# Four more gate columns computed by seven-product jobs ahead of the attention, eight instead of twelve computed directly inside it

## The chip, the cores and the metric

The kernel runs on one core of a Trainium2 chip. A core has five engines that run their own instruction streams in order and wait for each other on semaphores: PE (matrix multiply, 128x128, into eight PSUM banks), DVE (vector), ACT (scalar functions, copies, casts), POOL (GpSimd) and SP, which here only issues DMAs. The metric is the device time of one execution in microseconds (us); lower is better.

## The reference, cut to what matters

One decoder block, sequence 1024, width 1024, all in float32. The parts that matter here:

```
proj = xn @ w_in                       # (1024, 5136): q, k, v of two branches, code, gate_sb, gate_gla
o_sb  = stick_breaking_attention(...)  # 8 heads x 64, causal, blocks of 128 rows
o_gla = gla_chunked(...)               # 4 heads, then a norm and a swish gate
y = sigmoid(gate_sb + b_gate[0]) * (o_sb @ w_branch_sb) \
  + sigmoid(gate_gla + b_gate[1]) * (o_gla @ w_branch_gla)
h = x + y @ w_out                      # then a gated convolutional FFN and a last norm
```

The two merge gates are 2048 columns of `w_in`: sixteen "gates" of 128 columns each, numbered 0 to 15 (0 to 7 belong to the attention branch, 8 to 15 to the GLA branch). Each is a product of a 1024x128 weight with the 1024x1024 input, a bias and a sigmoid. The gates are needed only when the branches are merged, so they can be computed at any time before that.

## The kernel before, in words

Every float32 operand is split into a high and a low part of a rounded type (`split`, L118: a cast on ACT, then a subtraction on DVE at L110), and each product is three matmuls of these parts (`mac`, L189 to L197; every matmul of it is L195). The input is held transposed in four quarters, "11", "12", "21", "22" (512 rows of time by 512 of width).

Two ways lead to a gate.

- A **seven-product job** (`fast`, L225 to L303) computes two weights of 128 columns at once. It replaces the eight products of 512x512 blocks by seven, at the price of sums and differences of the weights (`first_pieces`, `more_pieces`) and of the products (the `add`s, L116) on DVE. A job is 7 x 12 = 84 matmuls of 128x512. The pairs come from `project_pairs` (L439): two pairs of GLA queries and keys, four of attention queries and keys, two of the swish gate, and then the first `N_GATES` of the sixteen gates, two by two. This is the stage of the pairs. In it a job's gate leaves over the sigmoid of L516, both halves at once.
- A **direct gate** (`gates`, L524 to L555) computes one weight of 128 columns in the plain way: two halves of time, each 24 matmuls in four steps of 6, then a sigmoid (L552) and a store (L553). It is a generator; each `fill(gate_steps, 1)` issues one step. The weights of a gate are cast and split once, or twice for the first `N_HALVES` = 3, whose two halves are computed far apart.

```
446        for g in range(0, N_GATES, 2):
447            yield tuple((C_GATE + n * P, gate_d, n * P) for n in (g, g + 1))
531        gs = range(N_GATES, 2 * NK)
532        order = [(g, (0,)) for g in gs[:N_HALVES]]
533        order += [(g, (0, 1)) for g in gs[N_HALVES:]] + [(g, (1,)) for g in gs[:N_HALVES]]
739    for w in attend():
740        owed += w + EACH
741        while owed >= FILL:
742            owed -= FILL
743            fill(gate_steps, 1)
939    fill(gate_steps, BEFORE)
```

The attention (`attend`, L687) runs in four rounds of two heads. A round goes through four quarters `tp` = 0 to 3; a quarter handles 256 rows of time for both heads, so its work grows with `tp`: 2, 4, 6 and 8 blocks of 128 keys. For a chunk of up to four blocks, `weigh` makes the logits on PE (L654), a sigmoid on ACT (L656), a mask on POOL where the chunk holds the diagonal (L658), and a running product from the right on DVE (L661, a scan). `turn_weights` transposes the result on PE (L668) and splits it (L119 on ACT, L110 on DVE); `gather` multiplies it with the values on PE (L677), ends with a bias on ACT (L682) and an add on DVE (L116), and stores. Chunks are transposed up to six chunks or twelve blocks after they were weighed. The first round also loads and splits the values (`value_blocks`, with POOL's L643) and reloads the quarter "21" of the input (`whole21`, L590, casts at L598).

The order of the instructions is fixed when the program is built. The attention hands out one step of a direct gate for each `FILL` blocks weighed, and in the second to seventh chunk of the first round one more each (`MORE`, L724). The matmuls of a step have a lowered priority (`LATER`, L545), and the scheduler that lays out PE's stream puts them between those of the attention. What is left over is issued after the attention (L939, L949), ahead of and between the first matmuls of `branch`, which multiplies the attention's output by `w_branch_sb` (L870) and reads the gates back.

Of the kernel before, what the change touches and what calls it, by code (L numbers as in the profile page):

```python
# [34 lines left out]
C_GATE = 3088  # L35
T2 = 11
T4 = 14
FILL = 3.6
EACH = 0
LATER = 25  # L40
MORE = 1
# [11 lines left out]
GLA = 2, 3  # L53
PACES = 0, 0, 0, 1
EARLY = 6
N_GATES = 4
AT_END = 51
N_READY = 1
N_OPS = 11
# [6 lines left out]
def block_kernel(ctx: ExitStack, tc: tile.TileContext, x, norm_mix_g, w_in, b_gate, w_alpha_up, b_alpha,  # L66
# [97 lines left out]
    def fill(steps, n):  # L164
        for _ in range(n):
            next(steps, None)
# [272 lines left out]
    def project_pairs():  # L439
# [4 lines left out]
        for j in range(0, 4, 2):  # L444
            yield tuple((C_GR + n * P, gr_d, n * P) for n in (j, j + 1))
        for g in range(0, N_GATES, 2):
            yield tuple((C_GATE + n * P, gate_d, n * P) for n in (g, g + 1))
# [76 lines left out]
    def gates():  # L524
# [5 lines left out]

        gs = range(N_GATES, 2 * NK)
        order = [(g, (0,)) for g in gs[:N_HALVES]]
# [206 lines left out]
    for w in attend():  # L739
        owed += w + EACH  # L740
        while owed >= FILL:
            owed -= FILL
            fill(gate_steps, 1)
# [528 lines left out]
```

## Time and profile before

| | us |
|---|---|
| median of 3 runs (lowest, highest) | 1415.81 (1415.05, 1417.85) |
| the profiled execution | 1416.46 |
| its span in the trace | 1414.7 |
| PE busy in the span | 1383.0 (98%) |
| DVE busy | 1061.3 (75%) |
| ACT busy | 650.7 (46%) |
| POOL busy | 108.2 (8%) |

The stage of the pairs begins at 113 us of the span and ends at 311 us with the first matmuls of the attention; the attention's last gather ends at 550 us. A busy PE is not yet a full one: matmuls overlap in the array, so that a 128x512 matmul is on record with some 390 ns while a stream of them takes less than 230 ns each. How full PE is, is read from how many matmuls pass in a stretch.

### The profile page before, as it was taken

How to read it: one execution, taken by the hardware profiler on the slowest of the kernel's cores; microseconds unless marked ns; L12 is line 12 of the kernel's file. 1: busy time of each engine (PE TensorE's matmuls, PEld its weight loads, DVE VectorE, ACT ScalarE, POOL GpSimd, SP SyncE). 2: the span in 40 equal slices, each digit the busy share in tenths (PEclk: the TensorE clock that was granted, in tenths of full speed). 3: DMA queues.
4: the chain of work that ended last, by engine and by line, in shares of the span. 5: the costliest groups of instructions: out<-in, count | busy, mean ns of one | idle time of the engine just before them, and what ended most of it. 6: DMA issues, size and time to landing. Idle time of an engine off the chain costs nothing.

```text
span 1414.7 us, 18378 instructions
## 1 busy us (share of the span) xinstructions
PE 1383.0 (98%) x6577; PEld 1143.1 (81%) x6577; DVE 1061.3 (75%) x1642; ACT 650.7 (46%) x1246; POOL 108.2 (8%) x190
## 2 busy tenths in 40 slices
PE   7999999998899999999999999999999999999997
PEld 6788888886788888878888788888888888888886
DVE  6387776766888876647446997998888987896765
ACT  6234334645766665643234543343333333554654
POOL 0000000003311110300000000000000000000000
PEclk9999999999999999999999999999999999999999
DMA  6332234376624436565324344564554437953332
GB/s 249 129 109 77 79 113 136 126 198 205 169 86 124 119 122 203 201 214 174 103 105 138 100 120 149 179 208 149 179 177 150 149 106 267 321 176 102 98 103 101
DMA packets 158397, 212.67 MB, mean 150 GB/s; under 512 B 9771, under 2 KB 103021, under 8 KB 157793
## 3 DMA queue, kind: packets, MB, share of 16 engines
q1 hardware_dynamic: 139696, 155.46, 35.8%
q0 software_dynamic: 11312, 41.48, 7.7%
q10 hardware_dynamic: 7296, 14.55, 2.8%
q8 instruction: 52, 0.85, 0.2%
q14 instruction: 41, 0.33, 0.1%
HBM read 153.65 MB, written 57.80 MB: 149 GB/s over the span
## 4 chain that ended last, share of the span: by engine, by line
PE 70%; DVE 2%; ACT 1%; issue 0%; DVEq 0%; ACTq 0%
PE bank L195 42%; PE bank L1135 15%; PE bank L1002 5%; PE bank L677 2%; PE bank L654 2%; PE bank L668 2%; DVE t L110 1%; DVE t L116 1%; PE bank L808 1%; PE bank L771 0%; PE bank L843 0%; PE bank L795 0%; PE bank L820 0%; PE bank L319 0%; DVE t L311 0%
## 5 line engine op out<-in xcount | busy, mean ns | idle before, releaser
L195 PE MATMUL bank<-t,t 128*128 128x512 f32 x3648 | 867.2, 393 | 3.6 <-DVE t L110 1.5
L195 PEld LDWEIGHTS bank<-t,t 128*128 128x128 f32 x3648 | 681.1, 188 | 150.4 <-DVE t L110 2.7
L110 DVE TENSOR_TENSOR t<-t,t 128x512 fp32r<-128x512 f32 (+2 forms) x651 | 430.3, 694 | 83.3 <-ACT t L119 78.1
L119 ACT CAST t<-t 128x512 fp32r<-128x512 f32 x537 | 311.1, 620 | 308.7 <-DVE t L110 67.7
L116 DVE TENSOR_TENSOR t<-bank,t 128x512 f32<-128x512 f32 (+1 forms) x284 | 182.8, 653 | 124.0 <-PE bank L195 60.5
L1135 PE MATMUL bank<-t,t 128*128 128x512 f32 x924 | 209.6, 389 | 0.0
L1135 PEld LDWEIGHTS bank<-t,t 128*128 128x128 f32 x924 | 173.4, 188 | 36.0
L110 DVE TENSOR_TENSOR t<-t 128x512 f32<-128x512 f32 (+1 forms) x124 | 88.0, 718 | 5.3 <-DMA t<-in_w_ffn_in_dram 3.5
L366 PE MATMUL bank<-t,t 128*128 128x512 f32 x384 | 91.4, 396 | 0.0
L1002 PE MATMUL bank<-t,t 128*128 128x512 f32 x384 | 88.9, 391 | 0.0
L110 DVE TENSOR_TENSOR t<-bank,t 128x512 fp32r<-128x512 f32 (+4 forms) x128 | 72.1, 576 | 22.2 <-ACT t L119 21.8
L1033 ACT ACTIVATE t<-t,vcol 128x1024 f32<-128x1024 f32 x22 | 27.4, 1245 | 128.0 <-DVE t L116 128.0
L366 PEld LDWEIGHTS bank<-t,t 128*128 128x128 f32 x384 | 72.4, 191 | 15.5 <-DVE t L110 0.4
L1002 PEld LDWEIGHTS bank<-t,t 128*128 128x128 f32 x384 | 71.6, 188 | 14.7
L116 DVE TENSOR_TENSOR t<-t,t 128x512 f32<-128x512 f32 x107 | 69.9, 684 | 16.1 <-ACT t L471 15.4
L119 ACT CAST t<-bank 128x512 fp32r<-128x512 f32 (+3 forms) x124 | 61.6, 510 | 40.7 <-PE bank L319 19.4
L661 DVE TENSOR_TENSOR_SCAN t<-t,zero 128x128 f32<-128x128 f32 (+1 forms) x64 | 54.5, 861 | 23.4 <-POOL t L658 23.2
L1035 DVE SCALAR_TENSOR_TENSOR t<-t,vcol,t 128x1023 f32<-128x1023 f32 (+1 forms) x44 | 56.2, 1278 | 14.1 <-ACT t L1033 13.9
L654 PE MATMUL bank<-t,t 128*128 128x128 f32 (+3 forms) x192 | 55.7, 368 | 1.6 <-DVE t L110 1.6
L668 PE MATMUL bank<-ident,t 128*128 128x128 f32 x288 | 52.2, 275 | 3.1 <-DVE t L661 1.2
L658 POOL TENSOR_SCALAR_AFFINE_SELECT t<-t 128x128 f32<-128x128 f32 x64 | 34.2, 540 | 192.2 <-ACT t L656 184.0
L677 PE MATMUL bank<-t,t 128*128 128x256 f32 (+1 forms) x320 | 45.8, 277 | 2.7 <-ACT t L119 1.9
(126 smaller groups left out, 768.4 us busy)
## 6 DMA issues: line engine op xcount, KB each, us to landing
t<-in_w_ffn_in_dram SPq DMA_DIRECT2D x50, 512.0 KB, 4.1
t<-in_w_in_dram SPq DMA_DIRECT2D x43, 512.0 KB, 5.3
act_d<-t POOLq DMA_DIRECT2D x22, 512.0 KB, 5.7
t<-in_w_ffn_out_dram SPq DMA_DIRECT2D x22, 512.0 KB, 5.5
wsum_d<-t POOLq DMA_DIRECT2D x22, 512.0 KB, 4.4
t<-act_d SPq DMA_DIRECT2D x22, 512.0 KB, 5.7
t<-wsum_d SPq DMA_DIRECT2D x44, 256.0 KB, 3.3
t<-sqk_d SPq DMA_DIRECT2D x40, 256.0 KB, 4.2
```

The source lines that it names most:

```text
L110: nc.vector.tensor_tensor(out=o, in0=a, in1=b, op=ALU.subtract)
L116: nc.vector.tensor_tensor(out=o, in0=a, in1=b, op=ALU.add)
L119: nc.scalar.copy(h, src)
L195: nc.tensor.matmul(pt, a[:, kk], b[:, kk], start=start and kk == 0 and m == 0, stop=stop and kk == k - 1 and m == 2)
L366: nc.tensor.matmul(pt, a[:, k % 4, t], b, start=k == 0 and m == 0, stop=k == NK - 1 and m == 2)
L654: nc.tensor.matmul(z[:, 0:w], q[:, a, e, ts_], kk[:, e, b0 * P:b1 * P], start=a == 0, stop=a == 1)
L661: nc.vector.tensor_tensor_scan(out=kr, data0=kr, data1=zero.to_broadcast([P, w]), initial=1.0 if right is None else right[:, 0:1], op0=ALU ...
L668: nc.tensor.transpose(pt[:, b * P:(b + 1) * P], ke[:, b * P:(b + 1) * P], ident)
L677: nc.tensor.matmul(po[:, c0:2 * P], vt[b][:, head, :], a[b // 4][:, b % 4, c0:], start=(b == 0 and n == 0), stop=(b == nb - 1 and n == 1))
L1002: nc.tensor.matmul(pt, a[:, k % 4, t], b, start=(k == 0 and m == 0), stop=(k == NK - 1 and m == 2))
L1035: nc.vector.scalar_tensor_tensor(out=cv[:, i:], in0=av[:, :S - i], scalar=col(V_CW, (2 - i) * NF + f), in1=cv[:, i:], op0=ALU.mult, op1=AL ...
L1135: nc.tensor.matmul(pts[m][i], a[:, t], b, start=(k == 0 and x_ == 0), stop=(k == NH - 1 and x_ == 2))
```

## The change

`N_GATES` goes from 4 to 8: gates 4 to 7 join gates 0 to 3 as pairs, so the stage of the pairs has twelve jobs instead of ten, and eight direct gates are left instead of twelve. `FILL` goes from 3.6 to 5.6, so that the fewer steps are spread over the whole attention. A direct gate has 48 matmuls (two halves of 24), so four of them have 192; two jobs have 168.

```diff
-FILL = 3.6
+FILL = 5.6
...
-N_GATES = 4
+N_GATES = 8
```

In steps of six matmuls: before, 97 steps (the first of which only loads), of which the attention hands out 88 and 8 are left for behind it; in the changed kernel 65, with 58 and 6. On the other engines the program as a whole has 28 more additions and subtractions of 128x512 on DVE, and on ACT six more casts, two more copies, four more sigmoids of 128x1024 and eight fewer of 128x512. SP's DMAs are the same in number.

The first place to look at is PE between two rounds of the attention, from the last gather of the second round (L677) to the first gather of the third. L668 are transposes, L654 logits, L195 here steps of a direct gate. Before:

```order
L677 MATMUL bank_4081<-t_673_3771,t_516_2990 128x128
L195 MATMUL bank_4020<-t_474_2799,t_680_3815 128x512
L195 MATMUL bank_4020<-t_475_2800,t_680_3815 128x512
L195 MATMUL bank_4020<-t_474_2799,t_680_3815 128x512
L668 MATMUL bank_4103<-ident,t_708_3955 128x128
L195 MATMUL bank_4020<-t_474_2799,t_680_3815 128x512
L195 MATMUL bank_4020<-t_475_2800,t_680_3815 128x512
L195 MATMUL bank_4020<-t_474_2799,t_680_3815 128x512
L654 MATMUL bank_4107<-t_654_3671,t_679_3806 128x512 x2
L668 MATMUL bank_4126<-ident,t_710_3971 128x128 x2
```

In the changed kernel, at the same place:

```order
L677 MATMUL bank_4229<-t_708_3955,t_558_3238 128x128
L668 MATMUL bank_4251<-ident,t_739_4118 128x128
L654 MATMUL bank_4255<-t_688_3859,t_714_3990 128x512 x2
L668 MATMUL bank_4274<-ident,t_741_4128 128x128 x2
L677 MATMUL bank_4279<-t_724_4049,t_458_2825 128x256
```

The attention's own matmuls stand in the same order; the six matmuls of a direct gate between them are gone. Counted over the whole attention, from its first logits to its last gather, there are 524 matmuls of direct gates before and 355 in the changed kernel. By rounds that is 174, 120, 120, 110 before and 126, 78, 72, 79 in the changed kernel; by quarters, 73, 29, 43, 29 against 54, 24, 25, 23 in the first round, 19, 24, 48, 29 against 6, 23, 25, 24 in the second, 19, 28, 44, 29 against 6, 19, 29, 18 in the third and 19, 24, 48, 19 against 13, 17, 31, 18 in the fourth.

The second place is PE behind the attention, where the last direct steps meet the first matmul of `branch` (the L195 row with a new bank and new weights at the end of each piece). L771 belongs to the GLA's states. Before:

```order
L195 MATMUL bank_5423<-t_474_2799,t_983_5361 128x512
L771 MATMUL bank_5455<-t_975_5333,t_974_5331 128x256
L195 MATMUL bank_5423<-t_475_2800,t_983_5361 128x512
L195 MATMUL bank_5423<-t_474_2799,t_983_5361 128x512 x2
L195 MATMUL bank_5423<-t_475_2800,t_983_5361 128x512
L195 MATMUL bank_5423<-t_474_2799,t_983_5361 128x512 x2
L195 MATMUL bank_5423<-t_475_2800,t_983_5361 128x512
L195 MATMUL bank_5423<-t_474_2799,t_983_5361 128x512 x2
L195 MATMUL bank_5423<-t_475_2800,t_983_5361 128x512
L195 MATMUL bank_5423<-t_474_2799,t_983_5361 128x512
L195 MATMUL bank_5423<-t_55_320,t_984_5364 128x512
L195 MATMUL bank_5466<-t_986_5382,t_999_5420 128x512
```

In the changed kernel:

```order
L195 MATMUL bank_5402<-t_516_3057,t_985_5327 128x512 x2
L195 MATMUL bank_5402<-t_517_3058,t_985_5327 128x512
L195 MATMUL bank_5402<-t_516_3057,t_985_5327 128x512
L195 MATMUL bank_5402<-t_55_320,t_986_5330 128x512
L195 MATMUL bank_5402<-t_56_321,t_986_5330 128x512
L195 MATMUL bank_5402<-t_55_320,t_986_5330 128x512 x2
L195 MATMUL bank_5402<-t_56_321,t_986_5330 128x512
L195 MATMUL bank_5402<-t_55_320,t_986_5330 128x512 x2
L195 MATMUL bank_5486<-t_1003_5415,t_1016_5453 128x512
```

Between the last gather and that first matmul of `branch` stand 41 matmuls of direct gates before and 24 in the changed kernel; behind it, before the branch is alone with the GLA, 11 and 5 more.

## Rows read from the trace of the kernel before

**Rows 1.** The page: busy time and share of the span.

```profile
PE 1383.0 (98%) x6577; PEld 1143.1 (81%) x6577; DVE 1061.3 (75%) x1642; ACT 650.7 (46%) x1246; POOL 108.2 (8%) x190
```

**Rows 2.** The page: the chain that ended last, by engine.

```profile
PE 70%; DVE 2%; ACT 1%; issue 0%; DVEq 0%; ACTq 0%
```

**Rows 3.** Windows: pairs, four rounds, tail; start:end us, length, busy by engine, PEclk.

```profile
113.00:311.00 198.00, 198.00 (x869) 160.95 (x867) 139.63 (x227) 92.19 (x145) 10.82 (x20) 1.00 0.40 118
311.10:393.50 82.40, 72.28 (x403) 59.08 (x402) 63.00 (x89) 52.52 (x108) 27.24 (x32) 1.00 0.65 190
393.50:447.10 53.60, 53.60 (x321) 46.53 (x321) 44.20 (x65) 35.80 (x79) 7.96 (x16) 1.00 0.38 104
447.10:500.70 53.60, 53.60 (x323) 46.52 (x321) 44.33 (x66) 32.80 (x75) 8.81 (x16) 1.00 0.39 114
500.70:550.00 49.30, 49.26 (x295) 42.39 (x294) 34.68 (x53) 28.62 (x65) 3.75 (x9) 1.00 0.45 142
550.00:568.30 18.30, 18.30 (x82) 15.11 (x81) 9.49 (x18) 9.43 (x17) 0.75 (x2) 1.00 0.81 261
```

**Rows 4.** Timeline of PE, two jobs of the pairs: start, length, count.

```profile
253.44 38.38 PE L195 MATMUL bank<-t,t 128*128 128x512 f32 x168
```

**Rows 5.** Windows: the third quarters of rounds two, three and four.

```profile
412.70:432.60 19.90, 19.90 (x114) 16.99 (x114) 18.28 (x25) 11.92 (x26) 3.30 (x5) 1.00 0.31 87
467.40:486.30 18.90, 18.90 (x110) 16.17 (x110) 16.44 (x23) 10.88 (x24) 2.51 (x4) 1.00 0.32 88
520.00:538.50 18.50, 18.50 (x103) 15.46 (x103) 16.75 (x24) 12.02 (x27) 2.31 (x5) 1.00 0.53 168
```

**Rows 6.** Groups of DVE in 311.1 to 550, by form: the splits.

```profile
L110 DVE TENSOR_TENSOR t<-t,t 128x512 fp32r<-128x512 f32 x35 | 25.0, 747 | 0.2 <-ACT t L119 0.2
```

**Rows 7.** Windows: the four quarters of the first round.

```profile
311.10:339.30 28.20, 24.14 (x126) 19.22 (x125) 20.45 (x30) 14.84 (x33) 12.74 (x15) 1.00 0.58 178
339.30:355.60 16.30, 13.78 (x78) 10.89 (x77) 8.04 (x13) 10.62 (x21) 2.77 (x3) 1.00 0.89 276
355.60:378.90 23.30, 19.76 (x111) 15.82 (x110) 22.46 (x28) 17.39 (x35) 8.38 (x7) 1.00 0.63 175
378.90:393.50 14.60, 14.60 (x97) 13.15 (x96) 12.04 (x20) 9.67 (x21) 3.35 (x7) 1.00 0.54 142
```

**Rows 8.** Waits, 339 to 356 us: waiter, releaser, total us, times, longest.

```profile
POOL t L643 <- DMA t<-sbv_d: 4.0, 1, 4.0
DVE t L116 <- ACT t L682: 3.9, 1, 3.9
ACT t L598 <- DMA t<-x_d: 3.5, 2, 2.2
```

**Rows 9.** Timeline of all engines behind the attention, in brackets idle before.

```profile
549.84 6.82 PE L195 MATMUL bank<-t,t 128*128 128x512 f32 x29
...
552.38 5.12 SPq L945 DMA_DIRECT2D t<-osb_d  x8
...
556.47 0.69 ACT L552 ACTIVATE t<-bank,vcol 128x512 f32<-128x512 f32 x1 [3.16 <-PE bank L195]
...
562.63 0.62 ACT L119 CAST t<-t 128x512 fp32r<-128x512 f32 x1 [0.41 <-DMA t<-osb_d]
```

**Rows 10.** Windows: two stretches of the FFN.

```profile
780.00:800.00 20.00, 19.22 (x87) 14.97 (x85) 20.00 (x35) 12.36 (x24) 0.00 (x0) 1.00 0.63 158
...
900.00:1000.00 100.00, 100.00 (x443) 82.78 (x442) 93.09 (x138) 37.36 (x56) 8.53 (x16) 1.00 0.53 178
```

**Rows 11.** Timeline of PE, a wait in the first round.

```profile
332.22 0.39 PE L677 MATMUL bank<-t,t 128*128 128x256 f32 x1 [1.93 <-ACT t L119]
```

**Rows 12.** Windows: six microseconds at the end of the GLA.

```profile
618.00:624.00 6.00, 3.32 (x13) 1.94 (x12) 2.30 (x5) 4.55 (x22) 0.00 (x0) 0.83 0.94 332
```

**Rows 13.** Timeline of PE in these microseconds.

```profile
622.65 0.77 PE L195 MATMUL bank<-t,t 128*128 128x512 f32 x1
```

## The prediction

> **What bounds the kernel now.** I read the page's busy shares first, then the chain, then windows cut at the stages. PE is busy 98% of the span, DVE 75% and ACT 46% [rows 1], and the chain that ended last is PE's to 70% where it is told apart [rows 2]; no other engine has more than 2%. So at first sight every matmul saved is time saved. The windows qualify that [rows 3]. In the stage of the pairs PE is busy for all of 198 us with DVE at 139.63 (71%). In the second and third round of the attention PE is also busy throughout, but DVE works 44.20 and 44.33 of 53.60 us (82% and 83%). There PE is full because direct gates are put between the attention's matmuls; the attention's own work is more DVE's than PE's. The reader is to see in these rows that the matmuls taken out of the attention come from the one stage in which a second engine stands close behind PE.
>
> The first round is different: 82.40 us, of which PE is busy 72.28. It has 10.1 us in which PE waits although gates are at hand.
>
> **The price of a matmul.** Two jobs, 168 matmuls, take 38.38 us in the stage of the pairs [rows 4]: 0.2285 us each. Direct gates are of the same form and PE is in a stream there too, so I use 0.2285 for both.
>
> **What is added.** Two jobs more in the stage of the pairs: +38.4 us on PE. Their sums on DVE, casts and sigmoids on ACT are hidden under PE as those of the ten jobs are (DVE 71%, ACT 92.19 of 198 us, 47% [rows 3]); a job like the others needs no more of them than the others. If that cover were gone, DVE would have to be over 100%, far from 71%. So +38.4 is firm.
>
> **What is removed.** Four direct gates, 192 matmuls, 43.9 us on PE; 169 of them lie in the attention and 23 behind it. If PE stayed full everywhere, the sum would be 24 matmuls or 5.5 us less. The question is how much of the 43.9 us comes back.
>
> *Rounds two to four* last 53.6 + 53.6 + 49.3 = 156.5 us. They lose 42, 48 and 31 direct matmuls, together 121 or 27.6 us of PE's work. DVE loses two splits of the gates' weights in each, at 0.75 us [rows 6], 4.5 us in all. I take each round in two parts, the third quarter, where DVE is densest, and the rest, and let the longer of the two engines set the time.
> - Second round: third quarter 19.9 us on PE less 23 x 0.2285 = 14.6; DVE 18.28 less two splits = 16.8 [rows 5]. DVE sets it: 16.8. The rest: 33.7 less 19 matmuls = 29.4, DVE there 25.9: 29.4. Together 46.2.
> - Third round: third quarter 18.9 less 15 matmuls = 15.5 on PE, DVE 16.4: 16.4. The rest: 34.7 less 33 matmuls = 27.2, DVE 27.9 less two splits = 26.4: 27.2. Together 43.6.
> - Fourth round: third quarter 18.5 less 17 matmuls = 14.6, DVE 16.75 less two splits = 15.3: 15.3. The rest: 30.8 less 14 matmuls = 27.6. Together 42.9.
>
> The sum is 132.7, so 23.8 us come back of 27.6. This supposes that DVE can be busy all the time where it is the bound. The trace has such a stretch: 780 to 800 us, DVE 20.00 of 20.00 with PE at 19.22 [rows 10]. The bounds: all 27.6 where the six waiting chunks even out the quarters, and 15.6 where two thirds of the 33.3 us in which DVE now idles in these rounds stay.
>
> *The first round* loses 48 direct matmuls, 11.0 us. By quarters [rows 7]: the first loses 19 (4.3 us), but PE already waits 4.1 us in it for values that are still being loaded and split, so I take half, 2.2. The second loses 5 (1.1 us); DVE works only 8.04 of 16.30 us and the waits there are for the values and for the reloaded quarter of the input, which come by DMA [rows 8]; I take 0.5. The third loses 18 (4.1 us), but DVE is busy 22.46 of 23.30, so 0.8 at most. The fourth loses 6 (1.4 us) with DVE at 12.04 of 14.60: all 1.4. Together 4.9, with bounds 2 and 11.0.
>
> *Behind the attention* 23 direct matmuls less are 5.3 us. They cover a round trip: the last output is stored, the outputs are loaded from 552.38 on, and the cast of the last one waits for its DMA until 562.63, though the attention's last gather ends at 550 [rows 9]. Of what stands ahead of the branch's first matmul, 17 matmuls (3.9 us) go. Some of this trip is PE's own doing, since ACT waits 3.16 us for a gate's bank ahead of those casts [rows 9], and that wait shortens with it. I take 4.0; bounds 1.4 (what goes later than the branch's start) and 5.3.
>
> **The sum.** +38.4 - 23.8 - 4.9 - 4.0 = +5.7 us. The profiled execution took 1416.46 us, 0.65 over the median of 1415.81; 1416.46 + 5.7 - 0.65 = 1421.5 us.
>
> [...] A wait of 1.93 us in the first round [rows 11] lies in a quarter with a granted clock of 1.00 [rows 7]. At the end of the GLA, after PE had done only 13 matmuls in six microseconds, the clock was 0.83, and a 128x512 matmul took 0.77 us [rows 12, 13]. [...]
>
> **The rivals.**
> - *PE stays the bound throughout.* As whole rounds, PE's work after the change (44.0, 42.6, 42.2 us) is still not below DVE's (42.7, 42.8, 33.2). In the FFN PE passes 443 matmuls in 100 us, as fast as anywhere, with DVE at 93.09 [rows 10]. If the chunks that wait between the engines even out the quarters and the first round's waits do not grow, all 43.9 us come back: 1415.81 - 5.5 = 1410.3 us, faster. Against it: DVE's 22.46 of 23.30 in one quarter of the first round [rows 7], where PE is already held back. It decides from 41.2 us given back on.
> - *Evened rounds, a stubborn first round.* Rounds two to four give all 27.6, the first 6 and the end 4.5: 38.1 back for 38.4 paid, 1416.1 us, no change.
> - *DVE's waits stay.* DVE waits for chains over ACT and POOL, such as 3.9 us for the bias of a gather [rows 8]. If two thirds of its idle time in rounds two to four stay (118.7 us of work and 22.2 us of waits), 15.6 come back there, 3 in the first round and 3 behind: +16.8, 1432.6 us. Against it: most of that idling is PE's, since gates stand between a chunk and its next step.
> - *The clock falls.* In rows 12 the clock was low for about a third of six microseconds, so some 1.0 us is lost each time. One such fall for each of the four rounds adds 4 to the forecast: 1425.5 us.
>
> **How the numbers follow.** About 0.2%, 2.8 us, is what a measurement of this kernel can tell from no change. I give the forecast 0.50 (its own spread of some 3 us leaves a sixth of that within 0.2%), PE bound throughout 0.14, evened rounds 0.18, waits that stay 0.13, the clock 0.05. Slower: 0.42 + 0.13 + 0.05 = 0.60. Within 0.2%: 0.08 + 0.14 = 0.22. Faster: 0.14 + 0.04 = 0.18. The range runs from 1411, which takes in most of the gain, to 1429, which stops short of the waits that stay; the forecast's own range is 1418 to 1425.
>
> **What would show it.** Right: a stage of the pairs of some 236 us with PE full; rounds two to four of 46, 44 and 43 us; third quarters in which DVE is busy to over 95% and PE waits for DVE's scans (L661) or splits (L110), which take a place in the chain that they do not have now; a first round of 77 to 78 us. The forecast is wrong on the fast side if the rounds last 44, 43 and 42 us with PE busy throughout, and on the slow side if they last 47 or more with DVE well under 95%. A granted clock below 1.00 inside the attention would show the last rival. If the stage of the pairs grew by other than 38 us, the one firm term would be wrong.

## The result, and the profile after

| | before | changed kernel |
|---|---|---|
| median of 6 runs each (lowest, highest), us | 1415.73 (1415.05, 1417.85) | 1423.09 (1422.39, 1424.21) |
| span of the profiled execution, us | 1414.7 | 1421.0 |
| PE, DVE busy in the span, us | 1383.0, 1061.3 | 1384.2, 1079.0 |

The changed kernel is slower: ratio 1.0050, 95% interval [1.0038, 1.0063], or 7.4 us in the medians and 6.3 us in the spans. It has 24 matmuls less, and yet PE is busy for a microsecond longer.

These are the windows of the changed kernel at the same stages as [rows 3]: the pairs, the four rounds, and the time to the same matmul behind the attention; the columns are those of [rows 3].

```profile
113.00:349.00 236.00, 236.00 (x1036) 192.24 (x1034) 162.18 (x263) 105.71 (x165) 10.79 (x20) 1.00 0.40 117
349.00:426.90 77.90, 64.97 (x353) 53.24 (x353) 63.19 (x87) 50.15 (x104) 27.37 (x32) 0.93 0.63 186
426.90:472.60 45.70, 44.81 (x280) 38.70 (x279) 42.19 (x63) 32.92 (x75) 10.36 (x16) 1.00 0.36 97
472.60:516.80 44.20, 43.40 (x275) 37.43 (x274) 42.11 (x64) 30.00 (x71) 8.19 (x16) 1.00 0.43 124
516.80:559.80 43.00, 42.63 (x266) 36.36 (x265) 34.36 (x55) 27.61 (x64) 6.72 (x9) 1.00 0.46 147
559.80:574.50 14.70, 14.01 (x60) 10.52 (x60) 7.95 (x16) 8.21 (x14) 0.70 (x2) 1.00 0.87 288
```

The stage of the pairs ends at 349.0 instead of 311.1: +37.9 us. The rounds last 77.9, 45.7, 44.2 and 43.0 us instead of 82.4, 53.6, 53.6 and 49.3: 4.5, 7.9, 9.4 and 6.3 us back. The time behind falls from 18.3 to 14.7: 3.6 back. Sum: +37.9 - 4.5 - 23.6 - 3.6 = +6.2 us, the difference of the spans but for 0.1. In rounds two and three DVE is now busy for 92% and 95%, and for the first time PE has waits there.

The third quarters of rounds two to four, to be held against [rows 5]:

```profile
443.10:458.30 15.20, 14.86 (x91) 12.73 (x91) 15.14 (x21) 8.93 (x20) 4.12 (x4) 1.00 0.34 97
...
487.90:503.70 15.80, 15.80 (x95) 13.14 (x95) 15.73 (x22) 9.98 (x22) 3.41 (x4) 1.00 0.28 78
...
533.70:549.00 15.30, 15.30 (x90) 12.65 (x90) 14.68 (x22) 10.02 (x23) 2.58 (x3) 1.00 0.33 94
```

DVE is busy 15.14 of 15.20, 15.73 of 15.80 and 14.68 of 15.30 us: it has next to nothing left there. PE is on record as busy nearly throughout as well. The four quarters of the first round, against [rows 7]:

```profile
349.00:376.30 27.30, 22.27 (x107) 18.01 (x107) 18.00 (x27) 13.24 (x30) 10.96 (x14) 0.87 0.58 179
376.30:390.50 14.20, 12.22 (x72) 9.85 (x70) 12.29 (x17) 12.45 (x26) 5.41 (x5) 1.00 0.86 280
390.50:411.00 20.50, 16.85 (x91) 13.64 (x91) 18.11 (x23) 13.35 (x27) 8.14 (x6) 0.92 0.58 161
411.00:426.90 15.90, 13.64 (x89) 11.74 (x88) 14.79 (x23) 11.12 (x24) 2.86 (x7) 1.00 0.59 147
```

PE waits in every quarter, 12.9 us in all where it waited 10.1 before, and the granted clock falls below 1.00 in two of them. Behind the attention, the timeline of PE and ACT (in brackets the idle time before and what ended it) shows the round trip of the attention's output, which was covered before:

```profile
565.09 0.62 ACT L119 CAST t<-t 128x512 fp32r<-128x512 f32 x1 [2.08 <-DMA t<-osb_d]
...
568.20 3.99 ACT L119 CAST t<-t 128x512 fp32r<-128x512 f32 x6 [1.31 <-DMA t<-osb_d]
...
568.87 0.50 PE L195 MATMUL bank<-t,t 128*128 128x512 f32 x1 [0.46 <-ACT t L119]
```

ACT, no longer held up by a gate's bank as in [rows 9], now waits for the DMA itself, and PE waits 0.46 us for ACT.

### The profile page after: what moved, and what is told of

Its sections match the earlier page's. It is cut to its first block, busy times and chain, and to the rows that moved or that the text cites. A ratio compares the mean times of both kernels' runs of the same rounds, so it can differ in the third digit from the quotient of the medians.

```text
span 1421.0 us, 18386 instructions
## 1 busy us (share of the span) xinstructions
PE 1384.2 (97%) x6553; PEld 1141.3 (80%) x6553; DVE 1079.0 (76%) x1670; ACT 654.0 (46%) x1250; POOL 113.4 (8%) x190
## 4 chain that ended last, share of the span: by engine, by line
PE 85%; issue 7%; DVE 3%; DMA 2%; POOL 1%; ACT 1%; SPq 0%; POOLq 0%; DVEq 0%; ACTq 0%
PE bank L195 53%; PE bank L1135 15%; PE bank L366 6%; PE bank L1002 5%; DVE t L110 2%; PE bank L677 1%; PE bank L654 1%; DMA t<-sbv_d 1%; PE bank L319 1%; PE bank L668 1%; POOL t L658 1%; DVE t L116 1%; PE bank L426 1%; PE bank L808 1%; DVE t L661 1%
## 5 line engine op out<-in xcount | busy, mean ns | idle before, releaser
L195 PE MATMUL bank<-t,t 128*128 128x512 f32 x3624 | 861.6, 393 | 1.7 <-DVE t L110 1.1
L195 PEld LDWEIGHTS bank<-t,t 128*128 128x128 f32 x3624 | 677.6, 188 | 148.3 <-DVE t L110 3.1
L110 DVE TENSOR_TENSOR t<-t,t 128x512 fp32r<-128x512 f32 (+1 forms) x661 | 437.2, 695 | 80.9 <-ACT t L119 73.9
L119 ACT CAST t<-t 128x512 fp32r<-128x512 f32 x543 | 314.8, 620 | 311.4 <-DVE t L110 69.0
L116 DVE TENSOR_TENSOR t<-bank,t 128x512 f32<-128x512 f32 (+1 forms) x298 | 192.6, 656 | 124.8 <-PE bank L195 76.1
L110 DVE TENSOR_TENSOR t<-t 128x512 f32<-128x512 f32 (+1 forms) x128 | 91.0, 719 | 10.1 <-ACT t L586 6.3
L110 DVE TENSOR_TENSOR t<-bank,t 128x512 fp32r<-128x512 f32 (+4 forms) x128 | 72.0, 574 | 22.7 <-ACT t L119 22.2
L366 PEld LDWEIGHTS bank<-t,t 128*128 128x128 f32 x384 | 72.4, 191 | 15.5 <-DVE t L110 0.4
L1002 PEld LDWEIGHTS bank<-t,t 128*128 128x128 f32 x384 | 71.6, 188 | 14.7
L116 DVE TENSOR_TENSOR t<-t,t 128x512 f32<-128x512 f32 x107 | 70.2, 688 | 16.1 <-ACT t L471 15.4
L668 PE MATMUL bank<-ident,t 128*128 128x128 f32 x288 | 52.5, 280 | 8.0 <-DVE t L661 3.6
L654 PE MATMUL bank<-t,t 128*128 128x128 f32 (+3 forms) x192 | 56.9, 381 | 2.6 <-DVE t L110 2.2
L658 POOL TENSOR_SCALAR_AFFINE_SELECT t<-t 128x128 f32<-128x128 f32 x64 | 39.3, 619 | 204.8 <-ACT t L656 185.9
L677 PE MATMUL bank<-t,t 128*128 128x256 f32 (+1 forms) x320 | 50.2, 280 | 4.1 <-DVE t L110 3.6
```

The costliest lines, as they stand in the source:

```text
L110: nc.vector.tensor_tensor(out=o, in0=a, in1=b, op=ALU.subtract)
L116: nc.vector.tensor_tensor(out=o, in0=a, in1=b, op=ALU.add)
L119: nc.scalar.copy(h, src)
L195: nc.tensor.matmul(pt, a[:, kk], b[:, kk], start=start and kk == 0 and m == 0, stop=stop and kk == k - 1 and m == 2)
L366: nc.tensor.matmul(pt, a[:, k % 4, t], b, start=k == 0 and m == 0, stop=k == NK - 1 and m == 2)
L654: nc.tensor.matmul(z[:, 0:w], q[:, a, e, ts_], kk[:, e, b0 * P:b1 * P], start=a == 0, stop=a == 1)
```

## The experiments

Times of different runs are compared by their ratio to the kernel before, which ran beside each; the changed kernel stands at 1.0050. Lengths of rounds are read from the windows of each kernel's profile, cut at the last gather of each round.

**One: the filling alone, without the added jobs.**

```diff
-FILL = 3.6
+FILL = 5.6
```

> The kernel before (four gates in the pairs, twelve direct) with the sparser filling of the changed kernel, FILL 5.6: the attention holds 355 direct matmuls as in the changed kernel, and the 169 that it no longer holds run behind it. Theory (the attention cannot shrink as much as its matmuls, since DVE is close behind PE): the attention lasts 211 us as in the changed kernel instead of 239, while 169 x 0.2285 = 38.6 us are added behind it, so about +10 us: 1426 us. Rival (the two added jobs of the pairs are what costs): no change, 1416 us.

1428.78 us, ratio 1.0084 [1.0068, 1.0100]: +12 us. Windows of its four rounds and of the time behind:

```profile
311.60:390.00 78.40, 67.33 (x351) 54.76 (x350) 63.20 (x87) 49.96 (x104) 28.87 (x32) 0.89 0.62 186
390.00:435.90 45.90, 45.15 (x282) 38.98 (x281) 41.94 (x63) 32.91 (x75) 9.71 (x16) 1.00 0.36 97
435.90:480.10 44.20, 43.15 (x270) 36.91 (x270) 41.62 (x63) 30.04 (x71) 8.14 (x16) 1.00 0.40 114
480.10:523.50 43.40, 42.97 (x268) 36.70 (x267) 33.57 (x53) 26.72 (x62) 5.81 (x9) 1.00 0.44 142
523.50:575.00 51.50, 51.50 (x229) 42.65 (x229) 14.21 (x25) 17.52 (x30) 0.74 (x2) 1.00 0.61 185
```

The rounds are those of the changed kernel within 0.5 us, though no job was added. So the loss is made in the attention: what is taken out of it costs its full time elsewhere and gives back less. Moved into the pairs, it costs 24 matmuls less than behind the attention, hence 1.0050 and not 1.0084.

**Two: half the change.**

```diff
-FILL = 3.6
+FILL = 4.4
...
-N_GATES = 4
+N_GATES = 6
```

> Half the change: six gates in the pairs, ten direct, FILL 4.4. Theory (in each quarter the longer of PE and DVE): +19.2 in the pairs; rounds two to four give back 13.4 of 15.1, the first round 2.3 of 5.5, the end 1.2: +2.3 us, 1418 us. If PE stayed the bound at this filling: -2.7 us, 1413 us. If the loss grew in proportion to the gates moved: half of 7.4, 1419.4 us.

1418.52 us, ratio 1.0014 [1.0006, 1.0022]: +2.0 us. Its rounds:

```profile
330.50:408.00 77.50, 68.78 (x377) 56.73 (x376) 61.52 (x86) 50.67 (x105) 27.34 (x32) 0.96 0.64 191
408.00:457.90 49.90, 48.88 (x300) 42.12 (x298) 43.13 (x65) 34.52 (x78) 8.00 (x16) 1.00 0.38 106
457.90:509.10 51.20, 50.09 (x304) 43.04 (x303) 44.63 (x68) 32.18 (x75) 7.83 (x16) 1.00 0.37 105
509.10:553.60 44.50, 44.19 (x273) 37.84 (x271) 33.35 (x51) 27.66 (x64) 4.13 (x9) 1.00 0.46 146
```

The ratio is that of the theory, +2.3, and excludes the 1413 us of a PE that stays the bound. The parts came out less well: rounds two to four gave back 10.9 us instead of 13.4, the first 4.9 instead of 2.3, so that the sum is right in part by luck. In rounds two and three PE waits 1.0 and 1.1 us although DVE is busy for only 86% and 87%; there neither engine's total sets the length. The half step loses less than half, by little more than the noise.

**Three and four: more work on DVE, in the kernel before and in the changed one.**

```diff
         split(ah, al, by(pt[:, 0:nb * P], nb))
+        if nb % 2:
+            sub(al, by(pt[:, 0:nb * P], nb), ah.bitcast(F32))
...
-        add(o[0:64, 0], po[0:64, 0:2 * P], o[0:64, 1])
+        for _ in range(2):
+            add(o[0:64, 0], po[0:64, 0:2 * P], o[0:64, 1])
```

> The kernel before with more work on DVE in the attention: the low part of the weights is computed twice where a chunk has one or three blocks, and the add at the end of each gather is done twice; 5.3 us more of DVE in each round, the same output. Theory (DVE has 17% of idle time in rounds two to four while PE is full): nearly free, 1 to 3 us in the first round, 1417 to 1418 us. Rival (the attention is held by the length of its chains, not by DVE's load): the same addition as in the changed kernel with this edit.

> The changed kernel with the same additional work on DVE, 5.3 us in each round. Theory (DVE is the bound in much of rounds one to three): 8 to 16 us slower than the changed kernel, about 1434 us, with rounds two and three of 48 us or more. Rival (the chains' length holds the attention): as little as in the kernel before with this edit, under 4 us, 1427 us at most.

The kernel before with it: 1418.67 us, ratio 1.0017 [1.0008, 1.0026], +2.4 us. The changed kernel with it: 1431.59 us, ratio 1.0110 [1.0096, 1.0124], 8.5 us more than the changed kernel (0.0060 of 1416). Rounds two and three of the first, then of the second:

```profile
395.40:449.70 54.30, 53.94 (x323) 46.69 (x322) 48.93 (x82) 35.53 (x79) 10.30 (x16) 1.00 0.38 103
449.70:503.90 54.20, 53.88 (x324) 46.78 (x322) 49.25 (x82) 32.79 (x75) 7.47 (x16) 1.00 0.38 113
```

```profile
428.30:477.80 49.50, 46.08 (x282) 38.60 (x281) 47.97 (x81) 33.23 (x75) 6.71 (x16) 1.00 0.33 91
477.80:525.20 47.40, 44.04 (x274) 37.60 (x274) 47.09 (x80) 30.60 (x71) 7.93 (x16) 1.00 0.40 115
```

Some 5 us more of DVE in a round lengthen it by 0.7 and 0.6 us before the change, by 3.8 and 3.2 us after it, where DVE is busy 97% and 99%. DVE had slack before and has little now. The 8.5 us are at the lower end of what I expected, and the third round stayed under the 48 us that I had named.

**Five and six: less work on DVE.** Left out are the subtraction that makes the keys' low part and the add that ends a gather, so the output is another.

```diff
             nc.scalar.copy(kk[:, e], kk[:, e].bitcast(F32))
             yield
-            sub(kk[other, e], raw[other], kk[other, e].bitcast(F32))
...
-        add(o[0:64, 0], po[0:64, 0:2 * P], o[0:64, 1])
```

> The changed kernel with less work on DVE in the attention and no more on any other engine: left out are the subtraction that makes the keys' low part (two of 1.2 us a round) and the add that ends each gather (eight of 0.33 us a round), 5 us of DVE in each round. Theory (DVE's load is the bound): rounds two and three get some 2 us shorter each, to PE's 44 and 43 us, the fourth under 1, the first up to 3: 5 to 8 us faster than the changed kernel, about 1417 us. Rival (the chains' length, not DVE's load): under 2 us.

> The kernel before with the same work left out. Theory (PE is the bound): no gain in rounds two to four, at most 2 us in the first: 1414 to 1416 us. Rival (less work on DVE is time won anywhere): as large a gain as in the changed kernel.

The changed kernel so cut: 1419.93 us, ratio 1.0032 [1.0020, 1.0045], 2.5 us less than the changed kernel. The kernel before so cut: 1413.47 us, ratio 0.9986 [0.9978, 0.9995], 2.0 us less. All four rounds of the first, and the first three of the second:

```profile
348.90:425.90 77.00, 65.78 (x353) 54.07 (x353) 58.91 (x79) 50.00 (x104) 26.29 (x32) 0.91 0.64 190
425.90:470.60 44.70, 44.24 (x281) 38.62 (x280) 38.36 (x54) 32.92 (x75) 7.91 (x16) 1.00 0.38 101
470.60:514.70 44.10, 43.23 (x275) 37.41 (x274) 36.59 (x52) 29.97 (x71) 7.02 (x16) 1.00 0.44 123
514.70:557.60 42.90, 42.63 (x265) 36.47 (x263) 31.84 (x46) 27.44 (x64) 3.87 (x9) 1.00 0.48 150
```

```profile
311.40:390.20 78.80, 71.07 (x400) 58.98 (x400) 60.33 (x81) 52.69 (x108) 23.88 (x32) 1.00 0.66 198
390.20:443.80 53.60, 53.60 (x322) 46.43 (x322) 39.90 (x55) 35.77 (x79) 6.34 (x16) 1.00 0.37 104
443.80:497.40 53.60, 53.60 (x323) 46.45 (x322) 39.64 (x56) 32.78 (x75) 6.61 (x16) 1.00 0.40 114
```

Before the change, rounds two and three keep their 53.60 us exactly: PE is the bound. After it, they gain 1.0 and 0.1 us and stop at 44.7 and 44.1, where PE is busy 99% and 98%. My 5 to 8 us were too much: I had counted 5 us of relief against 1.7 and 1.6 us that separate these rounds from PE's own work (44.0 and 42.6 us). The 2.5 us lie nearer to the rival's "under 2", and the two kernels gain about the same in all, as the rival of the second expectation had it; only the windows tell them apart, since the kernel before gains in its first round alone. So after the change PE is nearly full in rounds two to four as well, and less work on DVE gains little. What keeps the third round 1.5 us above PE's own work, with DVE busy for only 83%, is not DVE's load and was not found. And the changed kernel's first round hardly reacts: 0.9 us for 4.3 us less of DVE, where that of the kernel before gains 3.6. After the change DVE's load is not what holds it.

**Seven: the changed kernel without the masks on POOL** (the masking of the diagonal blocks is left out).

```diff
-        if right is None:
-            nc.gpsimd.affine_select(out=ke[:, w - P:w], in_=ke[:, w - P:w], pattern=[[-1, P]],
-                                    compare_op=ALU.is_gt, fill=1.0, base=0, channel_multiplier=1)
```

> The changed kernel without the masks on POOL (left out: the masking of the diagonal blocks), so that DVE's scan follows ACT's sigmoid directly; DVE's work is the same, the chain of each diagonal chunk is over half a microsecond shorter and no longer queues on POOL. Theory (DVE's load): little, under 3 us. Rival (the chains' length): 5 us or more faster than the changed kernel, 1418 us or less.

1422.10 us, ratio 1.0050 [1.0037, 1.0062]: no change. Rounds two to four last 45.0, 44.0 and 42.6 us, 1.3 us less together; the first lasts 79.2. The chain over POOL is not the bound of the changed kernel.

**Eight, nine, ten: DVE's subtractions for keys and queries on POOL**, in the changed kernel, with six gates, and in the kernel before.

```diff
-            sub(kk[other, e], raw[other], kk[other, e].bitcast(F32))
+            nc.gpsimd.tensor_tensor(out=kk[other, e], in0=raw[other], in1=kk[other, e].bitcast(F32), op=ALU.subtract)
...
-        sub(q[:, 1], q[:, 1].bitcast(F32), q[:, 0].bitcast(F32))
+        nc.gpsimd.tensor_tensor(out=q[:, 1], in0=q[:, 1].bitcast(F32), in1=q[:, 0].bitcast(F32), op=ALU.subtract)
```

> The changed kernel with the subtractions of the keys' and queries' low parts (four of 128x1024 or 64x1024 a round, some 1.2 us each) on POOL instead of DVE, the same output. Theory (DVE's load is the bound): DVE has 4.8 us less in each round, PE becomes the bound again with 44, 43 and 42 us: 3 to 5 us faster than the changed kernel, about 1419 us where the kernel before takes 1416. Against it: such a subtraction should take POOL over 3 us (its 128x512 takes 1.68), and the masks queue behind it. Rival (the chains' length is the bound): no gain, or slower by the masks' wait.

> Six gates in the pairs, ten direct, FILL 4.4, and the same subtractions on POOL. Theory: PE is the bound in rounds two to four, which then last some 48, 49 and 44 us, and of the 2.7 us that the two jobs save all but the first round's loss is kept: 2 to 3 us faster than six gates alone, 1415 to 1416 us, at best 1 us below the kernel before. Rival (chains): as six gates alone or slower.

> The kernel before with the same subtractions on POOL. Theory: PE is the bound, so DVE's relief gives nothing in rounds two to four and at most 1 us in the first: 1416 us. If the masks that queue behind POOL's subtractions matter, 1 to 3 us slower.

1436.51 us, ratio 1.0141 [1.0124, 1.0158]; 1427.74 us, ratio 1.0084 [1.0069, 1.0099]; 1424.83 us, ratio 1.0063 [1.0048, 1.0078]. All are slower, the kernel before too, by 9 us. POOL's groups in the first of the three (busy, mean ns, idle before):

```profile
L576 POOL TENSOR_TENSOR t<-t,t 64x1024 fp32r<-64x1024 f32 x8 | 22.4, 2796 | 9.7 <-ACT t L574 5.1 <-DMA t<-sqk_d 4.1
L588 POOL TENSOR_TENSOR t<-t 128x1024 fp32r<-128x1024 f32 x8 | 19.1, 2387 | 83.0 <-ACT t L586 83.0
```

A subtraction takes POOL 2.4 to 2.8 us, and the masks stand behind it in the same queue. What DVE's scans wait for the masks in rounds two and three (total us, times, longest), in this run and then in the changed kernel:

```profile
DVE t L661 <- POOL t L658: 13.7, 10, 4.6
```

```profile
DVE t L661 <- POOL t L658: 2.5, 6, 0.8
```

Rounds two and three grow to 48.4 and 47.2 us in the changed kernel and to 58.4 and 55.5 us in the kernel before. The gain I expected was wrong; the objection that stood beside it was what counted. In the kernel before, where I had expected 1 to 3 us from it at most, it cost 9. As a test of DVE's load these three tell nothing, since they lengthen a chain while they shorten a queue.

**Eleven: the changed kernel filled more sparsely.**

```diff
-FILL = 5.6
+FILL = 6.2
```

> The changed kernel with FILL 6.2: five steps, 30 matmuls, go from the attention to behind it. Theory (where DVE is the bound a gate taken out gives nothing back): +6.9 us behind, less 2 to 4 us in the attention and 1 us of the wait behind it: 2 to 4 us slower than the changed kernel, about 1426 us. Rival (the changed kernel is slow because its gates stand too densely at the wrong places): faster than the changed kernel.

1432.53 us, ratio 1.0117 [1.0102, 1.0132], 9.5 us slower than the changed kernel. Its rounds two and three:

```profile
425.50:472.50 47.00, 44.07 (x276) 37.26 (x275) 41.86 (x64) 32.00 (x73) 10.00 (x16) 1.00 0.41 109
472.50:519.00 46.50, 42.95 (x269) 36.14 (x269) 42.01 (x64) 31.07 (x74) 13.10 (x16) 1.00 0.34 96
```

The attention holds 323 direct matmuls instead of 355 and lasts 211.4 us instead of 210.8: 7.3 us of PE's work taken out give nothing back, and 8.4 us are added behind (23.1 us instead of 14.7). I had expected 2 to 4 us back. Rounds two and three even grow by 1.3 and 2.3 us while DVE is busy for only 89% and 90%, so here something other than DVE's total sets the time. PE's longest waits there are for DVE's subtractions (L110, 2.8 us) and adds (L116, 2.1 us), and the masks on POOL take 727 ns on average in these two rounds, 584 in the changed kernel. What makes these results late stays open; the place of the gates may matter as well as their number. That the changed kernel is slow because it is filled too densely is excluded.

**Twelve: the first round without the values' longer chain.** Left out are the second, shifted load of each block of values and POOL's subtraction, so the values are others.

```diff
-                raw, d = t2(), t2()
+                raw = t2()
                 nc.sync.dma_start(raw, sbv_d[i * P:(i + 1) * P, :])
...
-                nc.gpsimd.tensor_tensor(out=d, in0=d, in1=raw, op=ALU.subtract)
-                split(v2[:, i % 2, :, 0:SBD], v2[:, i % 2, :, SBD:P], d.rearrange("p (h d) -> p h d", h=SBH))
+                split(v2[:, i % 2, :, 0:SBD], v2[:, i % 2, :, SBD:P], raw.rearrange("p (h d) -> p h d", h=SBH))
```

> The changed kernel with the first round's preparation of the values shortened: left out are the second load of each block of values, shifted by a row, and POOL's subtraction of the two, so that ACT and DVE split a block as soon as its one load has landed. DVE and PE do the same work. Theory for the first round (it gives back 4.5 of 11.0 us because the values' chain over two DMAs and POOL holds it): the first round falls from 77.9 to 73 to 75 us, 3 to 5 us faster than the changed kernel. Rival (DVE's load or the lower clock holds it): the first round stays within 1.5 us.

1409.53 us, ratio 0.9954 [0.9940, 0.9967], 13.6 us less than the changed kernel. Its first round, and the first two quarters of that:

```profile
348.90:413.90 65.00, 60.27 (x352) 49.97 (x351) 55.61 (x86) 50.10 (x104) 19.28 (x23) 1.00 0.64 181
348.90:368.90 20.00, 19.15 (x107) 16.04 (x107) 15.57 (x28) 13.69 (x32) 4.76 (x9) 1.00 0.47 149
368.90:380.50 11.60, 11.60 (x72) 9.96 (x72) 9.23 (x16) 10.86 (x22) 1.74 (x2) 1.00 1.01 319
```

The first round falls by 12.9 us, with the clock at 1.00 throughout; the second lasts 45.6 us and stays where it was. That is some three times what I expected, and it shows where much of the first round's time is: in the loading and preparing of the values. The four quarters give 7.3, 2.6, 2.0 and 1.0 us of it, so the first two hold most. On PE's side, 8.2 us are waits (4.7 instead of 12.9) and 4.7 us are busy time (60.27 instead of 64.97, for 352 matmuls instead of 353), which goes with the clock of 1.00 instead of 0.93.

DVE is busy for 7.6 us less there although no instruction of DVE was left out. The scans of 128x384, which have all operands in SBUF (`t` or `zero` in the rows; a PSUM bank is `bank`), are shorter; in the first round of the changed kernel and then of this run (busy, mean ns, idle before):

```profile
L661 DVE TENSOR_TENSOR_SCAN t<-t,zero 128x384 f32<-128x384 f32 x6 | 7.8, 1298 | 6.0 <-POOL t L658 6.0
```

```profile
L655 DVE TENSOR_TENSOR_SCAN t<-t,zero 128x384 f32<-128x384 f32 x6 | 5.7, 944 | 0.2 <-POOL t L652 0.2
```

In the changed kernel two of the six scans, beside POOL's subtractions, take 2.04 and 1.95 us, the other four 0.94 to 0.96. Its subtractions of 128x512 that read one operand from a PSUM bank take 672 ns in the first round and 666 in rounds two to four, where POOL has masks alone. How the 8.2 us of waits are shared between the second loads, POOL's subtractions and DVE's longer instructions is not told apart. The same edit in the kernel before was not run. PE's waits in its first round are 10.1 us [rows 7], so it could gain no more than about that; whether the change would then pay stays open.

Of all versions here with the full output, the kernel before remains the fastest.

## Why the prediction was right, point by point

- **The pairs, +38.4.** Measured +37.9 from the start of the same window to the attention's first matmul. PE is full in all 236 us, as said.
- **Rounds two to four, 23.8 back of 27.6.** Measured 23.6, as 46.2, 43.6 and 42.9 forecast against 45.7, 44.2 and 43.0. The sum came out better than its parts. The forecast lost 3.8 us to DVE in the third quarters and nothing in the rest. The third quarters lasted 15.2, 15.8 and 15.3 us where 16.8, 16.4 and 15.3 were forecast, 1.6 us in all above PE's own 14.6, 15.5 and 14.6. The rest of these rounds lasted 30.5, 28.4 and 27.7 where 29.4, 27.2 and 27.6 were forecast, and lost 2.4. Experiments three and four show the mechanism, a second engine close behind PE: slack on DVE before, little after. That DVE's load alone takes the 4.0 us is not shown: with some 5 us less of it in each round, five brought back 1.2. And "the longer of two engines, in each part" did not hold with half the change (two) or with FILL 6.2 (eleven). So the agreement to 0.2 us is partly luck.
- **The first round, 4.9 back of 11.0.** Measured 4.5, but not by my quarters: 0.9, 2.1, 2.8 and -1.3 against 2.2, 0.5, 0.8 and 1.4. The size was right by luck, the reason half right. Of the 6.5 us lost, 2.8 are waits of PE (12.9 instead of 10.1). The other 3.7 are busy time: PE's fell by 7.3 us, from 72.28 to 64.97, where 48 matmuls less are 11.0, and the granted clock was 0.93; the sum had no term for that, only a rival had. I named DVE for the third quarter; five says that DVE's load counts for little in this round. The values' chain, which I had named for the first two quarters, is where twelve found most of its gain.
- **Behind the attention, 4.0 back of 5.3.** Measured 3.6. Of the 1.7 us lost, 0.7 are waits of PE in this window (14.01 busy of 14.70), where ACT's casts wait for the DMA of the attention's output.
- **The rivals.** PE as the bound throughout is excluded by one and two. Evened rounds would have given back 27.6 us in rounds two to four, not 23.6. Waits that stay as they were would have left these rounds at 141; they lasted 132.9. The lower clock did come, but only in the first round (0.93), not once in each. I estimate from PE's busy time that it is worth some 4 us there, 3.7 against the forecast and 4.7 against twelve; the rival had 1.0 us for one fall. It came together with the longer waits, and went with them in twelve.
- **The size.** +5.7 forecast, +6.2 by the windows, +7.4 in the medians. The two profiled executions, 1422.73 and 1416.46 us, are 6.3 us apart; the one lies 0.36 under its median and the other 0.73 over its own, which makes up the rest.

## What to carry to other kernels

Work that fills one engine's gaps in a stage cannot be taken out for more than the distance to the next engine there: read both engines' busy time in that stage's windows, part by part, and take the longer one as the least that each part can last. In the changed kernel rounds two to four lasted up to 1.7 us more than either engine's work. A saving of matmuls elsewhere has to be larger than what is lost at that floor; here 5.5 us saved met 12 us lost, about half of them in a round that was already held by its loads. Before a queue is relieved by moving work to an idle engine, look at what stands behind that work in the idle engine's own queue.

## What the runs showed of the hardware

In the changed kernel the 26 masks of 128x128 on POOL that ran beside no DVE instruction with all operands in SBUF took 0.28 to 0.29 us each, and the other 38 up to 2.01; in the kernel before 26 took 0.29 to 0.30 and 38 up to 1.38. From the run with FILL 6.2, the timeline of POOL and then that of DVE at the same time:

```profile
438.34 2.26 POOL L658 TENSOR_SCALAR_AFFINE_SELECT t<-t 128x128 f32<-128x128 f32 x1 [0.96 <-ACT t L656]
```

```profile
438.12 1.19 DVE L110 TENSOR_TENSOR t<-t 128x1024 fp32r<-128x1024 f32 x1
439.24 1.27 DVE L661 TENSOR_TENSOR_SCAN t<-t,t,zero 128x512 f32<-128x512 f32 x1
```

The mask starts 0.22 us after a DVE subtraction and ends at 440.60, 0.09 us after the scan behind it. It takes 2.26 us, where one at 429.97 us of the same run, with DVE idle, takes 0.29.

DVE's instructions were longer too. In the changed kernel's first round, the timeline of POOL and then that of DVE:

```profile
402.91 2.77 POOL L643 TENSOR_TENSOR t<-t,t 128x512 f32<-128x512 f32 x1
```

```profile
404.70 2.06 DVE L661 TENSOR_TENSOR_SCAN t<-t,t,zero 128x512 f32<-128x512 f32 x1
```

The scan starts while POOL's subtraction of the values runs and takes 2.06 us, where the one above takes 1.27. POOL's subtraction takes 2.77 us, where the shortest of its form in this round takes 1.28.

The granted clock fell twice in the changed kernel's first round, in its first quarter (0.87) and its third (0.92). The second time it was after a wait of PE for a scan. A window of it and the timeline of PE there:

```profile
404.00:408.00 4.00, 3.84 (x15) 2.53 (x14) 3.69 (x5) 2.24 (x6) 1.97 (x2) 0.66 0.33 121
```

```profile
402.99 0.78 PE L668 MATMUL bank<-ident,t 128*128 128x128 f32 x4 [3.49 <-DVE t L661]
403.42 1.20 PE L654 MATMUL bank<-t,t 128*128 128x512 f32 x2
...
407.54 0.72 PE L654 MATMUL bank<-t,t 128*128 128x512 f32 x2
```

After 3.49 us of waiting, two 128x512 matmuls take 1.20 us, and four microseconds later again 0.72; from 403.5 to 406 us the granted clock is 0.50, from 407 on 1.00. After the wait of 1.93 us in [rows 11] it stayed at 1.00 (332 to 340 us). In these runs the length of a wait does not settle it: in the changed kernel with the subtractions on POOL (experiment eight) matmuls soon were slower after a wait of 1.79 us (0.63 us for a 128x512, which took 0.40 at 466 us), and with FILL 6.2 they were not after 2.14 us (0.74 us for two). PE in the first and then in the second:

```profile
475.24 1.64 PE L677 MATMUL bank<-t,t 128*128 128x256 f32 x10 [1.79 <-DVE t L110]
476.67 0.63 PE L195 MATMUL bank<-t,t 128*128 128x512 f32 x1
```

```profile
448.67 0.74 PE L654 MATMUL bank<-t,t 128*128 128x512 f32 x2 [2.14 <-DVE t L116]
```

In rounds two to four of the changed kernel, where PE waits six times, each under 0.7 us, the clock stayed at 1.00.
